# Seven products for eight in the gate's first 512 columns and in one more column group of the MLP's second product

## The chip, the core and the metric

The kernel runs on one core of one Trainium2 chip, as one launch. The metric is the device time in microseconds (us). Before the change three runs took 2023.22, 2023.70 and 2024.14 us, with a median of 2023.7 us.

## The reference

Two layers work on 256 tokens of width 2048, in float32 with weights in float32:

```python
for l in range(2):
    h = rms_norm(x, norm1_g[l])                    # 256 x 2048
    z = h @ w_in[l]                                # 2048 x 5120
    q, k, v, gu, gv = split(z, 5 parts of 1024)
    attn = dilated_attention(rotary(q), rotary(k), v)          # 8 heads of 128
    gm = gelu(gu) * spatial(layer_norm(gelu(gv)))              # 8 groups of 128
    x = x + concat(attn, gm) @ w_out[l]            # 2048 x 2048
    h2 = rms_norm(x, norm2_g[l])
    x = x + square(relu(h2 @ w_up[l])) @ w_down[l] # 2048 x 8192, 8192 x 2048
out = rms_norm(x, final_g)
```

`layer_norm` is over each group's 128 columns, and `spatial` a masked 128x128 mixing of tokens.

## The kernel before

**Weights and products.** Weights stream from HBM in pieces of 128x1024 (`Sub`, L150). ACT rounds a piece to fp32r (`hi`, L168) and DVE subtracts that from it (`lo`, L178); the moving side is split likewise, and each product is three matmuls: hi·hi, lo·hi, hi·lo. There are 7 buffers for raw pieces, 6 for `hi` and 6 for `lo`.

**Three kinds of step.** A `transposed` step takes one piece and issues 24 matmuls of 256 columns (L410). A `natural` step takes one piece and issues 12 matmuls of 512 columns (L470 to L472). A `fast` product (L414) covers 512 columns by 1024 rows with seven products of half size, as Strassen's scheme has it, in two block-steps of 42 matmuls of 256 columns each (L440). `transposed` steps need 96 matmuls of 256 columns for the same, `natural` ones 48 of 512. A block-step takes two pieces, `Top` and `Bottom`. ACT and DVE split their left halves (the `Top` one 512 wide, L186 and L191). DVE makes four sums of 512 from the raw pieces (L219, L220, L223, L224), called raw sums below, and these go through ACT and DVE as two further pieces, `Sums`: the "upper" one after the first two raw sums, the "lower" one after the other two. The moving side needs sums too: `sums` (L800) makes them with four DVE operations of 512, and `to_half` (L644) splits them with one ACT and one DVE operation of 512 for each pair of chunks. A block's products use the left half of `Top`, the left half of `Bottom`, the right half of `Bottom`, then the upper sums (twice), then the lower ones.

**Order.** The program is a list of steps. Each engine runs its instructions in the order in which they are emitted. Before a step come the `hi` of pieces up to four ahead and the `lo` of pieces up to four ahead, then its matmuls, then the work that its results start (`after`), and then what `later` has queued, within a budget. `soon` puts a call ahead of a later step, `hook` and `mark` behind a given one.

**The input product, in both layers.** First v (16 natural steps), then k and q of two heads at a time (columns of 256, four transposed steps each: k0, q0, k1, q1 and so on, 32 steps in all), then gv (16 natural steps) and gu (transposed). When a k or q is done, ACT swaps its halves (L577, L578) and DVE applies the rotary (L579 to L581). Two steps after a q, `scores` (L587) runs: PE L593 (called s1) and L596 (s0), DVE L602 and L604, ACT exp L606. `normalise` (DVE L611, ACT L614) and `turn` (PE L622, ACT L624) follow some steps later. gv goes through a gelu, then `stats` and `layer_norm` on POOL (L686, L690), then the mixing.

**The MLP.** In nine eighths e = 0 to 8, `w_up` of eighth e and `w_down` of eighth e-1 are emitted together. The table `ORDER` (and `USUAL` for the eighths that it doesn't name) says which 512-column groups of `w_down` go by seven products, a pair of numbers each, and at which of the eighth's steps the two blocks stand. e = 1 has two groups, most others three. `put` (L870) adds a group's products into a buffer in HBM by DMA.

Of the kernel before, what the change touches and what calls it, by code (L numbers as in the profile page):

```python
# [59 lines left out]

ORDER = {1: ((7, 10), (13, 14)), 6: ((12, 15), (2, 3), (7, 8)), 7: ((7, 10), (2, 3)), 8: ()}
FINAL = (7, 7, 6)
LAST = (4, 6, 8, 10, 0, 2, 12, 14)
USUAL = ((7, 9), (2, 3), (13, 14))
WARM = 11
HALVES = 5
BEHIND, BETWEEN = 2, 1
D_SCORES, D_NORM, D_TURN, D_VALUES = 2, 1, 3, 2  # L70


# [19 lines left out]
def trunk(ctx: ExitStack, tc: tile.TileContext, layout, xT, consts, gains, w, b_sp, w_sp, out):  # L92
# [9 lines left out]
    paux = ctx.enter_context(tc.tile_pool(name="paux", bufs=4, space=bass.MemoryType.PSUM))  # L102

    vec, act, pe = nc.vector, nc.scalar, nc.tensor

# [29 lines left out]
    def acc_bank(i=None, of=4):  # L135
# [2 lines left out]
            i = bank_at[0] = (bank_at[0] + 1) % of  # L138
        return pacc.tile([P, 512], F32, name=f"acc{i}", tag=f"acc{i}")

    def aux_bank():
        return paux.tile([P, 512], F32, name="aux", tag="aux")


    class Sub:
# [268 lines left out]
    def fast(name, l, row0, col0, tiles, slots, fresh, last, done):  # L414

        o = []  # L420
        for p in range(2):
            top, bottom = (cls(name, l, row0 + (4 * h + 2 * p) * P, col0, 2, 512) for h, cls in enumerate((Top, Bottom)))
            upper, lower = Sums(top, bottom, False), Sums(top, bottom, True)

            def mm(p=p, top=top, bottom=bottom, upper=upper, lower=lower):
                if p == 0:
                    o.extend(slots())
                half = tiles[0][0]
                sums_ready()
                extra = sum_parts[0]  # L430
# [44 lines left out]
    def mark(fn):  # L475

        steps.append((None, fn, None))

    def from_hs(k):
        return hs[:, k, :, :]  # L480
# [37 lines left out]
    def layer(l, n1, n2, n3, last):  # L518
# [26 lines left out]

        if l:
            mark(start)
        mix_a, mix_g = [None], [None]
        qk = {}
        turned = []  # L550
# [104 lines left out]


        def after_gv(c, ps):
            z, u = t32("gz", [2, 512], tag="tmpB"), t32("gu", [2, 512], tag="tmpA")
            for tt in range(2):
                act.activation(z[:, tt, :], ps[tt], AF.Copy, scale=n1.half[:, tt:tt + 1])  # L660

            def then(u, z):
# [5 lines left out]
                later(1, 1.5, lambda: stats(c // P))  # L668

            gelu(z, u, then)  # L670

        def stats(g0):
# [8 lines left out]
            later(0, 1.0, lambda: layer_norm(g0))  # L681

        def layer_norm(g0):
            y, mv = par["y"], par["mv"]
            r = t32("lr", [2, 4])
            rsqrt(nc.gpsimd, r, mv[:, :, g0:g0 + 4, 1], 1.0, LN_EPS, [2, 4])  # L686
            for g in range(4):
                for tt in range(2):
                    yg = y[:, tt, (g0 + g) * P:(g0 + g + 1) * P]
                    nc.gpsimd.tensor_scalar(yg, yg, mv[:, tt, g0 + g, 0:1], r[:, tt, g:g + 1],  # L690
                                            op0=OP.subtract, op1=OP.mult)
            par["normed"] += 4

        def spatial(g0):
# [44 lines left out]
        hook(base + d + 3, n1.factor)  # L739
        hook(base + d + 6, rope)  # L740
        hook(base + d + 8, shift)
        for j in range(4):
            transposed("w_in", l, 0, KC, AW + j * 256, 256, from_hs, lambda c, ps, j=j: after_qk("k", j, ps))
            transposed("w_in", l, 0, KC, j * 256, 256, from_hs, lambda c, ps, j=j: after_qk("q", j, ps))
        natural("w_in", l, 4 * AW, AW, after_gv)
# [35 lines left out]
        def after_up(e):  # L781
            def f(c, ps):
# [6 lines left out]
                    vec.scalar_tensor_tensor(z, pair(ps), 0.0, wide(n2.R), op0=OP.max, op1=OP.mult)  # L789
                act.activation(z, z, AF.Square)  # L790
                to_half(hid[e][0], c // P, z, True)
                if c == 768:
                    summed[0] = False
                    if e == 0:
                        new_shared(F32R)
                        sum_parts[0] = shared[0].rearrange("p (k h t) -> p k h t", k=NH, h=2)
                    later(1, 1.5, sums)
            return f

        def sums():  # L800

            a11, a12, a21, a22 = (inner[:, 4 * k:4 * k + 4, t * P:(t + 1) * P] for t in range(2) for k in range(2))
            vec.tensor_tensor(a22, a21, a22, op=OP.add)
            vec.tensor_tensor(a21, a11, a21, op=OP.subtract)
            vec.tensor_tensor(a11, a22, a11, op=OP.subtract)
            vec.tensor_tensor(a12, a12, a11, op=OP.subtract)

            def parts(k):
                to_half(sum_parts[0], k, inner[:, k:k + 2, :])
                summed[0] = k == 6  # L810

            for k in range(0, 8, 2):
                later(0, 0.6, lambda k=k: parts(k))

        def combine(place, c, banks, o=None):

# [32 lines left out]
        def halves(bank):  # L849
            return [bank[:, 0:256], bank[:, 256:512]]  # L850

        held = []

        def sevenths():
# [58 lines left out]
        for e in range(9):  # L913
# [1 line left out]
            if e == 8:  # L915
                mark(lambda: bank_at.__setitem__(0, 1))
            if e < 8:
                up = collect(transposed, "w_up", l, 0, KC, e * 1024, 1024, from_hs, after_up(e), of=2)
            if e:
                w = 512 * len(ORDER.get(e, USUAL))  # L920
                hidden = [hid[e - 1]]
                down = collect(transposed, "w_down", l, (e - 1) * 1024, 8, w, D - w, from_tiles(hidden, NH),
                               lambda c, ps, e=e, w=w: after_down(e, (c + w) // P, ps),
                               apart=last and e == 8, of=2 if e < 8 else 4,
                               cols=None if e < 8 else [c * P for c in LAST])
                for g, at in enumerate(ORDER.get(e, USUAL)):
                    banks = []
                    quick += zip(at, collect(fast, "w_down", l, (e - 1) * 1024, 512 * g, hidden,
                                             (lambda g=g, banks=banks: slots_other(g, banks)) if g else slots_first,
                                             (0, 2, 4, 6) if g or e == 1 else (6,), range(7) if g or e == 7 else (6,),  # L930
                                             other_done(e, g, banks) if g else first_done(e)))
# [144 lines left out]
```

## Time and profile before

| | before |
|---|---|
| median of 3 runs | 2023.7 us (2023.22 to 2024.14) |
| the profiled execution | 2023.7 us, of which its span is 2021.9 us |
| PE busy | 2009.5 us (99%) |
| DVE busy | 1579.8 us (78%) |
| ACT busy | 1221.2 us (60%) |
| POOL busy | 156.2 us (8%) |
| granted PE clock, mean | 0.997 |

The 1.8 us between the execution and its span lie around the span. A row of the timeline or the chain gives a start in us from the span's start, then a duration. A group's "mean ns of one" is longer than the pace of a run of such instructions, since the next one starts before the last has ended; so paces are taken from the starts of neighbouring rows, and PE's from the chain of waits, which counts the time to the next start.

### The profile page before, as it was taken

To read this page: it belongs to the slowest core of one execution; us is meant where nothing else is said; L and a number is where in the kernel's file an instruction comes from. 1 tells how busy PE (TensorE), PEld (TensorE's weight loads), DVE (VectorE), ACT (ScalarE), POOL (GpSimd) and SP (SyncE) were. 2 spreads that over 40 slices of the span, in tenths; PEclk is the share of its full clock that TensorE was granted. 3 is DMA by queue.
4 is the path that set the end of the run, shared out by engine and by line. 5 is a ranking of instruction groups with operands and counts; after the bars stand their busy time and mean duration, and the time that the engine had idled before them with its cause. 6 is when DMAs were issued, how large, how long until landed. Compare 5 with 4: busy or idle time off the path is not lost.

```text
span 2021.9 us, 40716 instructions
## 1 busy us (share of the span) xinstructions
PE 2009.5 (99%) x16810; PEld 1973.4 (98%) x16810; DVE 1579.8 (78%) x1954; ACT 1221.2 (60%) x1613; POOL 156.2 (8%) x200
## 2 busy tenths in 40 slices
PE   9999999999999999999999999999999999999997
PEld 8998999999999999999989989999999999999997
DVE  7566766688888898898856667667888898888985
ACT  7565455566566666665645654556666666667653
POOL 0002300000001000100000032000000000010000
PEclk9999999999999999999999999999999999999998
DMA  9555556566678776866664555565676776777662
GB/s 330 192 167 167 187 189 202 174 229 204 222 219 239 240 225 203 249 215 215 201 215 158 168 187 188 188 199 179 217 229 208 228 236 216 239 220 241 212 215 81
DMA packets 126442, 419.26 MB, mean 207 GB/s; under 512 B 14128, under 2 KB 22064, under 8 KB 126256
## 3 DMA queue, kind: packets, MB, share of 16 engines
q1 hardware_dynamic: 110800, 389.86, 57.2%
q0 software_dynamic: 14304, 23.86, 6.5%
q8 instruction: 131, 2.15, 0.4%
q10 hardware_dynamic: 1152, 2.94, 0.4%
q14 instruction: 55, 0.45, 0.1%
HBM read 394.58 MB, written 22.02 MB: 206 GB/s over the span
## 4 chain that ended last, share of the span: by engine, by line
PE 99%; DVE 0%; ACT 0%; issue 0%; DVEq 0%
PE acc L410 70%; PE acc L440 10%; PE aux L440 8%; PE acc L470 3%; PE acc L472 3%; PE acc L471 3%; PE aux L699 0%; PE aux L635 0%; PE aux L593 0%; PE aux L622 0%; PE aux L994 0%; DVE x L1038 0%; PE aux L596 0%; PE aux L637 0%; PE acc L846 0%; PE aux L539 0%
## 5 line engine op out<-in xcount | busy, mean ns | idle before, releaser
L168 ACT ACTIVATE hi<-raw 128x1024 fp32r<-128x1024 f32 (+1 forms) x817 | 836.9, 1050 | 487.5 <-DVE raw L220 216.2
L178 DVE TENSOR_TENSOR lo<-raw,hi 128x1024 fp32r<-128x1024 f32 (+1 forms) x817 | 965.3, 1214 | 143.4 <-ACT hi L168 140.4
L410 PE MATMUL acc<-hs,hi 128*128 128x256 f32 x5632 | 985.9, 277 | 0.0
L410 PEld LDWEIGHTS acc<-hs,hi 128*128 128x128 f32 x5632 | 857.9, 188 | 0.4 <-issue 0.2
L410 PE MATMUL acc<-hs,lo 128*128 128x256 f32 x2816 | 778.0, 276 | 0.0
L410 PEld LDWEIGHTS acc<-hs,lo 128*128 128x128 f32 x2816 | 528.7, 188 | 0.4 <-issue 0.2
L410 PE MATMUL acc<-half,hi 128*128 128x256 f32 x2688 | 462.2, 276 | 0.0
L410 PEld LDWEIGHTS acc<-half,hi 128*128 128x128 f32 x2688 | 406.7, 188 | 0.0
L410 PE MATMUL acc<-half,lo 128*128 128x256 f32 x1344 | 371.0, 276 | 0.0
L410 PEld LDWEIGHTS acc<-half,lo 128*128 128x128 f32 x1344 | 252.3, 188 | 0.0
L873 POOL DMA_DIRECT2D far<-ar x92 | 74.2, 816 | 1164.4 <-ACT ar L876 563.9
L440 PE MATMUL acc<-hi,shared 128*128 128x256 f32 x768 | 138.4, 276 | 0.0
L440 PEld LDWEIGHTS acc<-hi,shared 128*128 128x128 f32 x768 | 119.2, 188 | 0.0
L440 PE MATMUL aux<-hi,half 128*128 128x256 f32 x528 | 110.6, 276 | 0.0
L440 PE MATMUL acc<-lo,shared 128*128 128x256 f32 x384 | 106.0, 276 | 0.0
L649 DVE TENSOR_TENSOR half<-ar,half 128x512 fp32r<-128x512 f32 x72 | 49.8, 691 | 68.6 <-ACT half L646 68.6
L470 PE MATMUL acc<-hi,hs 128*128 128x512 f32 x256 | 101.8, 398 | 0.0
L472 PE MATMUL acc<-hi,hs 128*128 128x512 f32 x256 | 100.6, 393 | 0.0
L471 PE MATMUL acc<-lo,hs 128*128 128x512 f32 x256 | 100.3, 392 | 0.0
L440 PEld LDWEIGHTS aux<-hi,half 128*128 128x128 f32 x528 | 87.2, 188 | 0.0
L440 PE MATMUL aux<-hi,shared 128*128 128x256 f32 x448 | 80.7, 276 | 0.0
L510 DVE TENSOR_TENSOR x<-x,acc 128x512 f32<-128x512 f32 (+1 forms) x49 | 33.1, 675 | 59.1 <-PE acc L410 57.3
(150 smaller groups left out, 1955.3 us busy)
## 6 DMA issues: line engine op xcount, KB each, us to landing
raw<-in_w SPq DMA_DIRECT2D x731, 512.0 KB, 4.7
far<-ar POOLq DMA_DIRECT2D x60, 256.0 KB, 8.3
far<-ar POOLq DMA_DIRECT2D x32, 128.0 KB, 4.3
ar<-far POOLq DMA_DIRECT2D x12, 256.0 KB, 9.7
raw<-in_w SPq DMA_DIRECT2D x10, 256.0 KB, 5.1
x<-in_xT SPq DMA_DIRECT2D x7, 256.0 KB, 5.9
out<-x SPq DMA_DIRECT2D x7, 256.0 KB, 3.1
shared<-in_b_sp ACTq DMA_DIRECT2D x2, 512.0 KB, 7.7
```

What stands on the lines that cost most here:

```text
L168: act.activation(self.h[:, j * m:(j + 1) * m], self.raw[:, j * m:(j + 1) * m], AF.Copy)
L178: vec.tensor_tensor(lo[:, r], self.raw[:, r], self.h[:, r].bitcast(F32), op=OP.subtract)
L410: pe.matmul(o, lhsT=lhs, rhs=xs[:, rhs, :], start=(first and j == 0), stop=(last and j == 2), skip_group_check=True)
L440: calls.append(lambda k=k, j=j, lhs=lhs, rhs=rhs: pe.matmul(o[n], lhsT=lhs, rhs=rhs, start=(p == 0 and k == 0 and j == 0 and n in fresh), ...
L470: pe.matmul(ps, lhsT=xh, rhs=hi, start=(k0 + k == 0), stop=False)
L471: pe.matmul(ps, lhsT=xh, rhs=lo, start=False, stop=False)
L472: pe.matmul(ps, lhsT=xl, rhs=hi, start=False, stop=(k0 + k == KC - 1))
L510: vec.tensor_tensor(xj, xj, ps[j][:, 0:S] if alone else pair(ps)[:, j, :], op=OP.add)
L649: vec.tensor_tensor(t[:, c:c + 2, 1, :], src, t[:, c:c + 2, 0, :].bitcast(F32), op=OP.subtract)
L873: nc.gpsimd.dma_start(far[g][:, r], src, **({} if e == max(g, 1) else {"accum_op": OP.add}))
```

## The change

1. In the MLP, eighth e = 1 has three groups by seven products where it had two: `ORDER[1]` gets the pair (7, 8), and the first group's blocks stand at 2 and 5. The eighth e = 0 makes its hidden columns in the order 0, 512, 256, 768 and its sums in two halves, and `put` writes at e = 1 where it added.
2. In the input product of both layers the first 512 columns of gv go by seven products, in four block-steps of `fast`, two for each half of the rows. They stand among the 32 steps of k and q: ahead of the steps counted 3 and 6 (first rows) and 16 and 24 (second rows) from zero; they are called block 3, 6, 16 and 24 below. For the moving side, `seven_sums` makes scaled copies of x (8 on ACT, of 256) and four DVE sums of 512 (both called plain), once in v's steps and once behind step 3, ahead of step 4. `seven_parts` splits them, four times for each rows. The products are gathered after block 24 by `gather` and go through the gelu (`gate_half`) in the late natural steps, of which 8 are left. k and q use two PSUM banks, and s0 goes to the other of these.
3. The first four groups' `layer_norm` runs on DVE instead of POOL, and the last `turn` comes a step earlier.

Over the program there are 772 matmuls of 128x512 before and 580 after, and 15704 of 128x256 before and 16016 after. The core of the diff:

```diff
-ORDER = {1: ((7, 10), (13, 14)), 6: ((12, 15), (2, 3), (7, 8)), 7: ((7, 10), (2, 3)), 8: ()}
+ORDER = {1: ((2, 5), (7, 8), (13, 14)), 6: ((12, 15), (2, 3), (7, 8)), 7: ((7, 10), (2, 3)), 8: ()}
...
+SEVEN, AGAIN = ((3, 6), (16, 24)), 8
...
+    def strassen_sums(f, i, n):
+
+        a11, a12, a21, a22 = (f[:, 4 * k + i:4 * k + i + n, t * P:(t + 1) * P] for t in range(2) for k in range(2))
+        vec.tensor_tensor(a22, a21, a22, op=OP.add)
+        vec.tensor_tensor(a21, a11, a21, op=OP.subtract)
+        vec.tensor_tensor(a11, a22, a11, op=OP.subtract)
+        vec.tensor_tensor(a12, a12, a11, op=OP.subtract)
...
-            s1, s0 = aux_bank(), aux_bank()
+            s1, s0 = aux_bank(), acc_bank(1 - bank_at[0]) if aux_held else aux_bank()
...
-            later(D_TURN, 0.5, lambda: turn(j, p1, p0))
+            later(D_TURN - (j == 3), 0.5, lambda: turn(j, p1, p0))
...
+        def seven_sums(rows):
...
+            f = seven["plain"][rows]
+            for k in range(NH):
+                c = NH * rows + k
+                act.activation(f[:, k, :], x[:, c, :], AF.Copy, scale=g_all[:, n1.g, c:c + 1])
+            strassen_sums(f, 0, 4)
+
+        def seven_parts(rows, k):
+            to_half(seven["sums"], k, seven["plain"][rows][:, k:k + 2, :])
+
+        def seven_done(o):
+            soon(5, lambda: gather(o))
...
             r = t32("lr", [2, 4])
-            rsqrt(nc.gpsimd, r, mv[:, :, g0:g0 + 4, 1], 1.0, LN_EPS, [2, 4])
+            e = nc.gpsimd if g0 else vec
+            rsqrt(e, r, mv[:, :, g0:g0 + 4, 1], 1.0, LN_EPS, [2, 4])
...
+        hook(base + 13, lambda: seven_sums(0))
+        for k in range(0, NH, 2):
+            hook(base + 14 + k // 2, lambda k=k: seven_parts(0, k))
...
+        quick = {}
+        for rows in range(2):
+            quick.update(zip(SEVEN[rows], collect(fast, "w_in", l, 1024 * rows, 4 * AW, seven_forms(rows), seven_slots,
+                                                  () if rows else (0, 2, 4, 6), range(7) if rows else (),
+                                                  seven_done if rows else None)))
...
+        for i, one in enumerate(plain):
+            if quick.get(i):
+                steps.append(quick[i])
+            if i == 4:
+                mark(lambda: seven_sums(1))
+            if AGAIN < i <= AGAIN + 4:
+                mark(lambda k=2 * (i - AGAIN - 1): seven_parts(1, k))
+            steps.append(one)
+        late = collect(natural, "w_in", l, 4 * AW + 512, 512, lambda c, ps: soon(1, lambda: after_gv(512, ps)))
...
+                if e == 0 and c == 512:
...
+                    later(1, 1.0, lambda: sums([0]))
...
-            nc.gpsimd.dma_start(far[g][:, r], src, **({} if e == max(g, 1) else {"accum_op": OP.add}))
+            nc.gpsimd.dma_start(far[g][:, r], src, **({} if e == 1 else {"accum_op": OP.add}))
```

Below, rows of the two programs stand in the order in which the engine runs them; lines of after have the changed file's numbers (there `hi` is L173 and `lo` L183, the rotary L594 to L596, the plain sums L485 to L488, the raw sums L224 to L229, and `half<-plain` the splitting of sums, L661 and L664).

On DVE in layer 0, from the last raw pieces of v to the rotary of k0, before has:

```order
L178 TENSOR_TENSOR lo<-raw,hi 128x1024 x2
L543 SCALAR_TENSOR_TENSOR shared<-aux,cols,shared 128x128 x8
L178 TENSOR_TENSOR lo<-raw,hi 128x1024 x2
L579 TENSOR_TENSOR ar<-acc_565,cosR 128x512
L580 TENSOR_TENSOR ar<-ar,sinR 128x512
L581 TENSOR_TENSOR ar<-ar 128x512
L178 TENSOR_TENSOR lo<-raw,hi 128x1024 x4
```

and after has, from the raw sums of block 6 to the `lo` of its upper sums, the first of eight:

```order
L224 TENSOR_TENSOR raw<-raw 128x2x256
L225 TENSOR_TENSOR raw<-raw 128x2x256
L228 TENSOR_TENSOR raw<-raw 128x2x256
L229 TENSOR_TENSOR raw<-raw 128x2x256
L594 TENSOR_TENSOR ar<-acc_583,cosR 128x512
L595 TENSOR_TENSOR ar<-ar,sinR 128x512
L596 TENSOR_TENSOR ar<-ar 128x512
L485 TENSOR_TENSOR plain<-plain 128x4x128
L486 TENSOR_TENSOR plain<-plain 128x4x128
L487 TENSOR_TENSOR plain<-plain 128x4x128
L488 TENSOR_TENSOR plain<-plain 128x4x128
L183 TENSOR_TENSOR lo<-raw,hi 128x1024 x8
```

Block 6's raw sums now stand ahead of k0's rotary and the second rows' plain sums behind it, and the `lo` of block 6's upper sums behind both.

On ACT at the same place before has:

```order
L168 ACTIVATE hi<-raw 128x1024 x4
L577 ACTIVATE ar<-acc_565 64x512
L578 ACTIVATE ar<-acc_565 64x512
L168 ACTIVATE hi<-raw 128x1024 x4
L577 ACTIVATE ar<-acc_703 64x512
L578 ACTIVATE ar<-acc_703 64x512
```

and after has, from block 3's `Sums` on, with the eight scaled copies (L717) behind k0's two copies:

```order
L173 ACTIVATE hi<-raw 128x1024 x3
L191 ACTIVATE hi<-raw 128x512
L173 ACTIVATE hi<-raw 128x1024 x2
L592 ACTIVATE ar<-acc_583 64x512
L593 ACTIVATE ar<-acc_583 64x512
L717 ACTIVATE plain<-x,cols 128x256 x8
L173 ACTIVATE hi<-raw 128x1024 x8
L592 ACTIVATE ar<-acc_807 64x512
L593 ACTIVATE ar<-acc_807 64x512
```

What moved: k0's copies stand behind the `hi` of block 6's upper sums, and that waits for DVE's raw sums.

On DVE behind the first scores of layer 0, before has:

```order
L178 TENSOR_TENSOR lo<-raw,hi 128x1024
L611 RECIPROCAL den<-den 128x4
L178 TENSOR_TENSOR lo<-raw,hi 128x1024
L579 TENSOR_TENSOR ar<-acc_829,cosR 128x512
L580 TENSOR_TENSOR ar<-ar,sinR 128x512
L581 TENSOR_TENSOR ar<-ar 128x512
L178 TENSOR_TENSOR lo<-raw,hi 128x1024 x4
```

and after has, from k1's rotary to q1's, with block 16's pieces in between:

```order
L183 TENSOR_TENSOR lo<-raw,hi 128x1024
L594 TENSOR_TENSOR ar<-acc_999,cosR 128x512
L595 TENSOR_TENSOR ar<-ar,sinR 128x512
L596 TENSOR_TENSOR ar<-ar 128x512
L664 TENSOR_TENSOR half<-plain,half 128x2x256
L196 TENSOR_TENSOR lo<-raw,hi 128x512
L183 TENSOR_TENSOR lo<-raw,hi 128x1024
L224 TENSOR_TENSOR raw<-raw 128x2x256
L225 TENSOR_TENSOR raw<-raw 128x2x256
L228 TENSOR_TENSOR raw<-raw 128x2x256
L229 TENSOR_TENSOR raw<-raw 128x2x256
L183 TENSOR_TENSOR lo<-raw,hi 128x1024 x2
```

Block 16's raw sums and the `lo` of both its `Sums` stand between the two rotaries, and what block 16's next step waits for stands behind the second.

## Rows read from the trace of the kernel before

**Rows 1.** Page, part 1 and the start of part 4: busy time; chain that ended last.

```profile
PE 2009.5 (99%) x16810; PEld 1973.4 (98%) x16810; DVE 1579.8 (78%) x1954; ACT 1221.2 (60%) x1613; POOL 156.2 (8%) x200
...
PE 99%; DVE 0%; ACT 0%; issue 0%; DVEq 0%
```

**Rows 2.** Windows: stretch, length, busy us (instructions) of each engine, clock, DMA.

```profile
50.00:250.00 200.00, 200.00 (x1522) 190.01 (x1521) 131.56 (x191) 110.17 (x164) 30.87 (x42) 1.00 0.55 178
390.00:560.00 170.00, 170.00 (x1501) 170.00 (x1500) 145.91 (x165) 108.84 (x135) 9.56 (x15) 1.00 0.65 213
```

**Rows 3.** Chain, layer 0: start us, us, what.

```profile
57.07 1.72 PE aux L539 x4
...
81.88 11.31 PE acc L410 x96
93.19 0.65 PE aux L622 x6
93.84 10.90 PE acc L410 x96
```

**Rows 4.** Chain in the MLP: a seven-product block.

```profile
466.61 4.08 PE acc L440 x36
```

**Rows 5.** Timeline of PE, first natural steps: start us, us, instruction.

```profile
7.87 0.39 PE L470 MATMUL acc<-hi,hs 128*128 128x512 f32 x1
...
11.99 0.39 PE L470 MATMUL acc<-hi,hs 128*128 128x512 f32 x1
```

**Rows 6.** Timeline of DVE in the MLP: the four raw sums and what follows.

```profile
469.61 0.69 DVE L219 TENSOR_TENSOR raw<-raw 128x512 f32<-128x512 f32 x1
...
472.39 2.52 DVE L178 TENSOR_TENSOR lo<-raw,hi 128x1024 fp32r<-128x1024 f32 x2
```

**Rows 7.** Lines by form, POOL: busy us, mean ns of one.

```profile
L690 POOL TENSOR_SCALAR shared<-shared,mv,lr 128x128 f32<-128x128 f32 x32 | 39.6, 1248 | 0.4
```

**Rows 8.** Timeline of DVE, layer 0, before and after the first steps on k.

```profile
45.08 4.63 DVE L178 TENSOR_TENSOR lo<-raw,hi 128x1024 fp32r<-128x1024 f32 x4
...
52.20 0.42 DVE L567 TENSOR_TENSOR cosR<-con,aux 128x256 f32<-128x256 f32 x1 [2.49 <-ACT nR L333]
...
52.94 2.36 DVE L178 TENSOR_TENSOR lo<-raw,hi 128x1024 fp32r<-128x1024 f32 x2
...
57.97 2.16 DVE L543 SCALAR_TENSOR_TENSOR shared<-aux,cols,shared 128x128 f32<-128x128 f32 x8 [2.67 <-PE aux L539]
```

**Rows 9.** Timeline of ACT: one pair of scaled copies of x.

```profile
300.35 0.91 ACT L287 ACTIVATE hs<-x,cols 128x256 fp32r<-128x256 f32 x2 [2.33 <-DVE x L510]
301.17 0.62 ACT L300 ACTIVATE nsq<-x 128x512 f32<-128x512 f32 x1
```

**Rows 10.** Timeline of ACT, layer 1: copies of q, then probabilities.

```profile
1064.77 0.60 ACT L577 ACTIVATE ar<-acc 64x512 f32<-64x512 f32 x1 [1.66 <-PE acc L410]
...
1083.41 0.51 ACT L606 ACTIVATE ar<-ar,mx 128x256 f32<-128x256 f32 x1 [3.97 <-DVE mx L604]
...
1085.18 1.04 ACT L168 ACTIVATE hi<-raw 128x1024 fp32r<-128x1024 f32 x1
1086.13 1.48 ACT L614 ACTIVATE ar<-ar,den 128x256 f32<-128x256 f32 x4
1087.52 1.04 ACT L168 ACTIVATE hi<-raw 128x1024 fp32r<-128x1024 f32 x1
```

**Rows 11.** Timeline of DVE, layer 1: rotary of q, then scores.

```profile
1066.02 0.69 DVE L579 TENSOR_TENSOR ar<-acc,cosR 128x512 f32<-128x512 f32 x1 [4.37 <-ACT ar L578]
...
1067.95 4.62 DVE L178 TENSOR_TENSOR lo<-raw,hi 128x1024 fp32r<-128x1024 f32 x4
...
1081.96 0.69 DVE L602 SCALAR_TENSOR_TENSOR ar<-aux,con 128x512 f32<-128x512 f32 x1 [0.72 <-PE aux L593]
...
1084.08 1.21 DVE L178 TENSOR_TENSOR lo<-raw,hi 128x1024 fp32r<-128x1024 f32 x1
```

**Rows 12.** Windows: near the end of the program.

```profile
2010.00:2015.00 5.00, 1.17 (x4) 0.88 (x4) 3.66 (x10) 0.00 (x0) 0.00 (x0) 0.57 0.26 86
```

More of the change, by code (lines that the diff above doesn't have):

```diff
@@ L101, in trunk @@
     pacc = ctx.enter_context(tc.tile_pool(name="pacc", bufs=1, space=bass.MemoryType.PSUM))
-    paux = ctx.enter_context(tc.tile_pool(name="paux", bufs=4, space=bass.MemoryType.PSUM))
+    paux = ctx.enter_context(tc.tile_pool(name="paux", bufs=1, space=bass.MemoryType.PSUM))
     vec, act, pe = nc.vector, nc.scalar, nc.tensor
@@ L139, in acc_bank @@
         return pacc.tile([P, 512], F32, name=f"acc{i}", tag=f"acc{i}")
+    aux_at, aux_held = [3], set()
     def aux_bank():
-        return paux.tile([P, 512], F32, name="aux", tag="aux")
+        i = next(j % 4 for j in range(aux_at[0] + 1, aux_at[0] + 5) if j % 4 not in aux_held)
+        aux_at[0] = i
+        return paux.tile([P, 512], F32, name=f"aux{i}", tag=f"aux{i}")
     class Sub:
@@ L412, in transposed, with fast @@
             steps.append((wt, mm, (lambda c=c: after(c, accs[c])) if k0 + 4 == nk else None))
-    def fast(name, l, row0, col0, tiles, slots, fresh, last, done):
+    def fast(name, l, row0, col0, forms, slots, fresh, last, done):
         o = []
@@ L427, in mm @@
                     o.extend(slots())
-                half = tiles[0][0]
-                sums_ready()
-                extra = sum_parts[0]
+                half, extra = forms()
                 left, right = slice(0, 256), slice(256, 512)
@@ L477, in mark, with halves @@
         steps.append((None, fn, None))
+    def strassen_sums(f, i, n):
[4 more added lines that the diff above has]
+        vec.tensor_tensor(a12, a12, a11, op=OP.subtract)
+    def halves(bank):
+        return [bank[:, 0:256], bank[:, 256:512]]
     def from_hs(k):
@@ L667, in then, with seven_slots @@
                 vec.scalar_tensor_tensor(par["y"][:, :, c:c + 512], u, 1.0, z, op0=OP.add, op1=OP.mult)
-                later(1, 1.5, lambda: stats(c // P))
+                if c:
+                    later(1, 1.5, lambda: stats(c // P))
+                else:
+                    stats(0)
             gelu(z, u, then)
+        seven = {}
+        def seven_slots():
+            if "o" not in seven:
+                banks = [acc_bank(2), acc_bank(3)]
+                for _ in range(2):
+                    banks.append(aux_bank())
+                    seven.setdefault("aux", []).append(aux_at[0])
+                aux_held.update(seven["aux"])
+                seven["o"] = [h for b in banks for h in halves(b)][0:7]
+            return seven["o"]
@@ new lines, in seven_forms @@
+        def seven_forms(rows):
+            return lambda: (hs[:, NH * rows:NH * (rows + 1)], seven["sums"])
+        def seven_sums(rows):
+            if "sums" not in seven:
+                f = tp.tile([P, 2, NH, S], F32, name="plain", tag="half", bufs=2)
+                seven["plain"] = [f[:, i, :, :] for i in range(2)]
+                seven["sums"] = tp.tile([P, NH, 2, S], F32R, name="half", tag="half", bufs=2)
+            f = seven["plain"][rows]
[3 more added lines that the diff above has]
+            strassen_sums(f, 0, 4)
@@ new lines, in seven_parts, with gather @@
+        def seven_parts(rows, k):
+            to_half(seven["sums"], k, seven["plain"][rows][:, k:k + 2, :])
+        def seven_done(o):
+            soon(5, lambda: gather(o))
+        def gather(o):
+            z = t32("gz", [2, 512], tag="tmpB")
+            p1, p2, p3, p5, p7, p6, p4 = o
+            c11, c12, c21, c22 = (z[:, tt, h * S:(h + 1) * S] for tt in range(2) for h in range(2))
+            act.activation(c12, p1, AF.Copy)
+            vec.tensor_tensor(c11, c12, p2, op=OP.add)
+            vec.tensor_tensor(c12, c12, p6, op=OP.add)
+            vec.tensor_tensor(c22, c12, p7, op=OP.add)
+            vec.tensor_tensor(c12, c12, p5, op=OP.add)
+            vec.tensor_tensor(c21, c22, p4, op=OP.subtract)
+            vec.tensor_tensor(c12, c12, p3, op=OP.add)
+            vec.tensor_tensor(c22, c22, p5, op=OP.add)
+            for tt in range(2):
+                act.activation(z[:, tt, :], z[:, tt, :], AF.Copy, scale=n1.half[:, tt:tt + 1])
+            aux_held.clear()
+            seven["z"] = z
@@ L680, in stats @@
                     vec.bn_aggr(mv[:, tt, g0 + g, :], st[:, tt, g, :])
-            later(0, 1.0, lambda: layer_norm(g0))
+            if g0:
+                later(0, 1.0, lambda: layer_norm(g0))
+            else:
+                soon(1, lambda: layer_norm(0))
         def layer_norm(g0):
@@ L741, in layer @@
         hook(base + d + 8, shift)
+        hook(base + 13, lambda: seven_sums(0))
+        for k in range(0, NH, 2):
+            hook(base + 14 + k // 2, lambda k=k: seven_parts(0, k))
+        plain = []
         for j in range(4):
-            transposed("w_in", l, 0, KC, AW + j * 256, 256, from_hs, lambda c, ps, j=j: after_qk("k", j, ps))
-            transposed("w_in", l, 0, KC, j * 256, 256, from_hs, lambda c, ps, j=j: after_qk("q", j, ps))
-        natural("w_in", l, 4 * AW, AW, after_gv)
+            for name, col in (("k", AW), ("q", 0)):
+                plain += collect(transposed, "w_in", l, 0, KC, col + j * 256, 256, from_hs,
+                                 lambda c, ps, j=j, name=name: after_qk(name, j, ps), of=2)
+        quick = {}
[3 more added lines that the diff above has]
+                                                  seven_done if rows else None)))
+        if l:
+            mark(lambda: bank_at.__setitem__(0, 1))
+        for i, one in enumerate(plain):
[7 more added lines that the diff above has]
+        late = collect(natural, "w_in", l, 4 * AW + 512, 512, lambda c, ps: soon(1, lambda: after_gv(512, ps)))
+        for i, one in enumerate(late):
+            if i == 5:
+                mark(lambda: gate_half(0, seven["z"]))
+            steps.append(one)
         transposed("w_in", l, 0, KC, 3 * AW, AW, from_hs, after_gu)
@@ L791, in f, with sums @@
                 to_half(hid[e][0], c // P, z, True)
+                if e == 0 and c == 512:
+                    new_shared(F32R)
+                    sum_parts[0] = shared[0].rearrange("p (k h t) -> p k h t", k=NH, h=2)
+                    later(1, 1.0, lambda: sums([0]))
                 if c == 768:
                     summed[0] = False
[L794 to L797, printed above, removed]
-            return f
[L800 to L806, printed above, removed]
+                    later(1, 1.5, lambda: sums([0, 1] if e else [1]))
+            return f
+        def sums(ps):
+            strassen_sums(inner, 2 * ps[0], 2 * len(ps))
             def parts(k):
@@ L812, in sums @@
             for k in range(0, 8, 2):
-                later(0, 0.6, lambda k=k: parts(k))
+                if k % 4 // 2 in ps:
+                    later(0, 0.6, lambda k=k: parts(k))
         def combine(place, c, banks, o=None):
@@ L917, in layer @@
             if e < 8:
-                up = collect(transposed, "w_up", l, 0, KC, e * 1024, 1024, from_hs, after_up(e), of=2)
+                up = collect(transposed, "w_up", l, 0, KC, e * 1024, 1024, from_hs, after_up(e), of=2,
+                             cols=None if e else (0, 512, 256, 768))
             if e:
```

17 lines of the change are left out of this document (11 added, 6 removed).

## The prediction

> **What bounds the kernel now.** I read the page first. PE is busy for 2009.5 of 2021.9 us, DVE for 78% and ACT for 60%, and the chain of work that ended last is PE for 99% [rows 1]. So a matmul that is saved is worth its pace, as long as nothing else becomes late. Next the windows. In the stretch of layer 0 that holds k, q and gv, PE is busy for 200.00 of 200.00 us, DVE for 131.56 (66%) and ACT for 110.17 (55%). In a stretch of the MLP in which most column groups go by seven products already, PE is busy for all of 170.00 us beside a DVE at 145.91 (86%) [rows 2]. The reader is to see that a fuller DVE doesn't by itself stop PE. It stops PE where a chain of DVE and ACT work ends later than PE comes to it, which is why the rest goes by places.
>
> **The matmuls.** The chain gives the pace of 256-column matmuls: 96 in 10.90 us, 0.1135 us each [rows 3]. In a seven-product block 36 take 4.08 us, the same 0.113 [rows 4], so a block of 42 takes 4.77 and a transposed step of 24 takes 2.725. The natural steps' 512-column matmuls start 18 apart between 7.87 and 11.99 us, 0.2289 each [rows 5]. The gate loses 96 of these per layer, 21.97 us, and gets 168 of 256 columns, 19.07 us: 2.90 us saved, 5.8 in two layers. The new group in the MLP has 84 matmuls for 96 per layer: 12 x 0.1135, in two layers 2.7. In sum 192 x 0.2289 - 312 x 0.1135 = 43.95 - 35.41 = **8.5 us saved**. Against the profiled execution's own 2023.7 us (a span of 2021.9 and 1.8 around it; the median of the runs is 2023.7 too) that gives 2015.2.
>
> **What DVE gets.** Per layer the k, q and gv stretch gets, on DVE, 16 raw sums, 8 plain sums and 8 splittings of 512 (0.695 each, four raw sums taking 2.78 us [rows 6]: 22.2 us), 4 `lo` of 1024 net (1.16 each, four in 4.63 [rows 8]: 4.6) and 4 of 512 (at 0.69, 2.8), and about 7.5 us of gathering and layer norm: 37 us. In 200 us that lifts DVE from 66% to 84%. The layer norm of four groups leaves POOL, where one operation takes 1.25 us [rows 7]. On DVE no row has it; L543, also of 128x128, took 2.16 / 8 = 0.27 us each [rows 8], and I take that. At POOL's price the 8 would take 10 us, at worst 7.8 us more of DVE, far from any matmul. The weights loaded are the same bytes. The raw pieces are held longer, but PE waits nowhere for a load in these windows, and I cost this at nothing.
>
> **Place 1: block 6 in layer 0.** From 45.08 us [rows 8], when DVE has ended the first norm, the new order has 10 `lo` of 1024 (11.6 us), 2 of 512 (1.4), 16 operations of 512 (11.1), cos and sin (0.74, from 52.20 to 52.94) and L543's eight (2.16) until block 6's raw sums are done: 27.0 us, so 72.1, if it never waits. Its upper two are done at 70.7. ACT then makes their `hi` (0.95 to 1.04 [rows 10], 71.7), k0's two copies (1064.77 to 1066.02 for q in layer 1, 1.25 [rows 10, 11], to 72.9) and the eight scaled copies. A pair of these moves the next start by 0.82 us [rows 9], so eight take 3.3: 76.2. Only then can DVE make the plain sums (2.78, to 79.0) and the `lo` of the upper sums (1.16, to 80.1). PE's own time: step 2 starts at 58.79 (57.07 and 1.72 more [rows 3]), step 2, block 3 and steps 3 to 5 bring it to 58.79 + 4 x 2.725 + 4.77 = 74.45, and after 19 matmuls of block 6 (2.16) it wants that `lo` at 76.6. It waits **3.5 us**. A DVE without the backlog would leave place 2's 0.9; if DVE also waits for ACT on the way, 4.5.
>
> **Place 2: block 6 in layer 1.** Here the first norm is done early and DVE has no backlog. Let step 3 end at e. k0's copies end at e + 1.25, with the `hi` of block 6 partly in front at e + 1.8. Eight copies: e + 5.1; plain sums: e + 7.9; `lo`: e + 9.0. PE wants it after steps 4 and 5 and 19 matmuls, at e + 7.6. It waits **1.4 us**; 0.9 if the `hi` isn't in front, 2.0 if all of it is.
>
> **Place 3: the step behind block 16, both layers.** The clock starts when s1 is done (1081.96 in layer 1 [rows 11]). PE then has s0 (0.44), six steps (16.35, of which four run 0.41 slower in before: 11.31 for 10.90), a turn (0.66 [rows 3]), block 16 (4.77), and two left-over matmuls and one of its own ahead of the first that needs the step's `lo`: 22.9. On DVE: the scores end at 2.1 [rows 11], a `lo` at 3.3. The splitting of sums waits for ACT, whose exps end at 3.2 (1085.18 less 1081.96 [rows 10]) and which makes a `hi` before its own part: 4.8, so DVE is at 5.6 with the reciprocal. A `lo` to 6.8. The next splitting waits for L614's four (1.39 to the next start [rows 10]), a `hi` and its ACT part: 8.6, done 9.3. A `lo`, k1's rotary (1066.02 to 1067.95, 1.93 [rows 11]), the last splitting, a `lo` of 512 and one of 1024: 14.9. Raw sums: 17.7, the upper `lo` 18.8. The lower `hi` on ACT stands behind the turn's copies and ends at 19.1, its `lo` at 20.3. On ACT one more `hi` and q1's two copies follow: 21.3. Then q1's rotary on DVE, 23.2, and the `lo` that PE wants, **24.4: 1.5 us late**, in each layer. If q1's copies could follow PE's last matmul (17.9) at once, they would end at 19.1 and nothing would be late; with the prices of single instructions for those of runs, it is up to 2.5.
>
> **The other places.** Behind each of these waits of PE stand only PE's own later matmuls; DVE and ACT don't wait for them in the next 5 us and catch up meanwhile, so the waits add up and don't spread. Block 3 is met with about 1 us to spare in layer 0, block 24 and the step behind it with 0.5, by the same count (the halves' splitting is over by then, which relieves DVE of 0.7 us in each of four steps, and ACT of as much). Behind block 24 the gather's 1 copy, 7 additions and 2 scalings stand off PE's path, with 2 us to spare at the next natural steps. In the MLP the pairs (2, 5), (7, 8) and (13, 14) put 9 us more on DVE in one eighth (8 raw sums, 2 `lo` of each width), a load which rows 2 show elsewhere with PE busy throughout: I cost them at 0, at most 1.5 us per layer. POOL issues 8 more DMAs for the third group, on a queue that is busy for 8% of the span [rows 1]; 0. `put` without adding, s0's other bank and the hidden columns' new order change no count on PE; 0.
>
> **The sum.** 2023.7 - 8.5 + 3.5 + 1.4 + 2 x 1.5 = **2023.1 us**. Bounds: 2015.2 + 0.9 + 0.9 = 2017.0 with only the smallest waits, 2015.2 + 4.5 + 2.0 + 5.0 + 3.0 = 2029.7 with the largest.
>
> **Rivals.** A, the waits are mostly hidden, with 0.9 left at places 1 and 2 and none at place 3: 2015.2 + 1.8 = **2017.0**. For it: DVE at 86% in the MLP beside a PE that never waits [rows 2], and queued work that runs ahead of what my counts allow; against it, places 1 and 2 hold a chain of k0's copies, eight copies and four sums in which only the 1.3 us of the `hi` and the backlog can shrink.
>
> B, slower: DVE's backlog isn't worked off between the blocks. Each of the waits on ACT in place 3 pushes the raw sums, they push the next `hi`, and the next block starts late too. Then place 1 costs 4.5, block 3 of layer 0 another 1.0, place 2 costs 2.0, and blocks 16 and 24 cost 2.0 each in both layers, 8.0: 2015.2 + 15.5 = **2030.7**. It decides from the point where the `lo` behind block 24 is over 0.5 us later than counted. For it: DVE's 84% with three engines taking turns; against it, the queues have 4.8 us of a block's matmuls to catch up in, and in the MLP they do.
>
> C, the clock falls in place 1. Before holds PE at a granted clock of 1.00 in both windows, where it never idles [rows 2]; between 2010 and 2015 us, where it works for 1.17 of 5.00, the mean is 0.57, a stretch at the lower level (1.2 of 2.4 GHz) for the most part [rows 12]. No row has a wait of 3.5 us in the midst of work. If the 23 matmuls left in block 6 ran at half pace, that is 2.6 us more: **2025.7**; half pace through the next step would add 2.7. The Trainium skill ("TensorE: Matmul & The Clock Gate", section on oscillation in real kernels) says that a wait of the matmul engine that is long enough halves its clock, and that what follows starts slow each time. By it, C's 2025.7 would hold if the wait is long enough; the trace agrees as far as its end goes.
>
> **How the numbers follow.** A difference of 0.2%, 4 us, is about what a measurement tells from no change, so faster is under 2019.7 and slower over 2027.7. My forecast with its neighbours, 2019.7 to 2025.5: 0.37. C: 0.06, also within. A and what lies between it and the forecast's lower side: 0.34. B with the upper bounds: 0.23. So faster 0.34, same 0.43, slower 0.23. The range goes from 2015.2, nothing late, to 2029.5; 0.05 lies below, 0.12 above. The forecast's own range is 2019.5 to 2026.
>
> **What would show it.** The waits of PE would name DVE's `lo` as releaser, with some 3.5 us once in layer 0 near 77 us and about 1.5 us at three more places; the chain would pass over the scaled copies and plain sums at block 6. PE's busy time should fall by 8.5 us, that of DVE rise by some 80. The forecast is wrong if PE has no wait over 1 us (A), or if waits of over 1 us stand at block 24 or behind (B), or if the granted clock falls below 1.00 near 80 us (C).

## The result, and the profile after

The change made the kernel slower: 2028.94 us median (2026.49 to 2030.13, 11 runs) against 2023.47 us of before; the ratio is 1.0026, with a 95% interval of 1.0018 to 1.0033. The forecast was 2023.1. Before's median is over 11 runs too, one of which took 5273.57 us, while the other ten lie between 2023.16 and 2024.14. The profiled execution has a span of 2028.4 us, 6.5 more than before's. At 2030.13 us it is the slowest of after's 11 runs, 1.2 us over their median, so what is read from it below adds up to that run and not to the median.

The page's first part, with busy time, share and instructions of each engine, answers to [rows 1]:

```profile
PE 2008.5 (99%) x16930; PEld 1979.2 (98%) x16930; DVE 1659.2 (82%) x2108; ACT 1258.8 (62%) x1695; POOL 136.8 (7%) x166
```

DVE is at 82% where it was at 78%: 79 us more, as forecast. PE's busy time has fallen by 1.0 us only, not 8.5, so its matmuls take longer too. The waits of PE, by what released it (us in total, times, longest):

```profile
PE acc L443 <- DVE lo L183: 6.3, 2, 3.3
PE aux L608 <- DVE ar L596: 1.2, 2, 0.6
```

Both lines are new. The first is block 6, once in each layer; the second is the first scores, once in each layer.

Where the 6.5 us come from can be read from one landmark, the first matmul of `w_out`. It starts at 244.12 us in before and at 249.03 in after: layer 0's input product is 4.9 us longer where 2.9 were to be saved, so 7.8 us are lost there. In layer 1 it starts 8.1 us late, after 3.6 at that layer's first norm (1018.07 and 1021.66): 4.5 longer, 7.4 lost. In between, the MLP gives back 1.3 us, and from layer 1's landmark to the end of the span 1.6: its 12 matmuls (1.36 us), in full.

**Block 6, 5.0 us in layer 0.** The chain of after there (start us, us, what):

```profile
74.58 1.39 PE acc L443 x13
...
75.99 0.70 DVE plain L485
...
78.17 0.04 DVE plain L488
...
78.78 1.23 DVE lo L183
...
80.05 0.84 PE acc L443 x5
80.89 2.94 PE aux L443 x16
83.83 0.21 PE acc L415
84.05 0.43 PE aux L443 x2
84.47 5.52 PE acc L415 x47
```

PE runs dry, and the chain goes over DVE's plain sums and the upper `lo`, which ends at 80.0. The prediction had 80.1. From 74.58 to 84.47 are 43 matmuls, counting six that ran beside the plain sums, 4.88 us at 0.1135; they took 9.89. Of the 5.0 us, 3.3 are the wait. The other 1.7 lie behind it: the last 24 matmuls took 80.05 to 84.47, 4.42 us for 2.72, at up to 0.21 us each, and then the pace is 0.1135 again. The window there (length, busy us of PE, PEld, DVE, ACT and POOL, clock):

```profile
80.00:84.40 4.40, 4.35 (x25) 4.35 (x26) 4.40 (x4) 1.75 (x2) 0.00 (x0) 0.65 0.65 196
```

The granted clock is 0.65 in this stretch, part of it at the lower level of 1.2 GHz, after 3.3 us in which PE did nothing. It doesn't fall with the restart: the matmuls up to 81.18 still start 0.11 to 0.12 us apart (the first two 0.22), those from 81.29 on 0.21. In layer 1 the same block took 4.9 us too long, 3.0 by the wait and 1.9 behind it.

**The first scores, 1.0 us.** The chain of layer 0 behind block 6:

```profile
93.32 1.13 PE aux L608 x4
94.45 0.45 PE acc L611 x4
94.89 13.62 PE acc L415 x120
108.52 0.66 PE aux L637 x6
109.17 5.46 PE acc L415 x48
114.63 2.72 PE acc L443 x24
```

s1 starts at 93.32; 71 matmuls after 84.47 would have brought it to 92.5, and its four take 1.13 us where they take 0.87 in the other scores. Then come 120 matmuls, a turn and 48 more before block 16 at 114.63: seven steps, not six.

**The pace, 1.4 us.** One place of before has 96 matmuls in 11.31 us [rows 3]. The chain of after, later in layer 0:

```profile
124.91 11.31 PE acc L415 x96
136.22 0.65 PE aux L637 x6
136.88 8.48 PE acc L415 x72
```

That is 0.1178 each, at a granted clock of 1.00. In before it holds for 96 matmuls of each layer, in after for some 420, from block 16's end to the last scores: 420 x 0.0043 = 1.8 us for 0.4. The three together are 7.4 of the 7.8 us.

### The profile page after: what moved, and what is told of

Its sections match the earlier page's. It is cut to its first block, busy times and chain, and to the rows that moved or that the text cites. A ratio compares the mean times of both kernels' runs of the same rounds, so it can differ in the third digit from the quotient of the medians.

```text
span 2028.4 us, 41171 instructions
## 1 busy us (share of the span) xinstructions
PE 2008.5 (99%) x16930; PEld 1979.2 (98%) x16930; DVE 1659.2 (82%) x2108; ACT 1258.8 (62%) x1695; POOL 136.8 (7%) x166
## 4 chain that ended last, share of the span: by engine, by line
PE 98%; DVE 1%; DMA 1%; ACT 0%; issue 0%; ACTq 0%; DVEq 0%; SPq 0%
PE acc L415 69%; PE acc L443 11%; PE aux L443 9%; PE acc L475 2%; PE acc L473 2%; PE acc L474 2%; PE aux L608 0%; PE aux L774 0%; PE aux L650 0%; DMA raw<-in_w 0%; PE aux L637 0%; DMA x<-in_xT 0%; DVE x L1138 0%; PE aux L652 0%; PE acc L943 0%
## 5 line engine op out<-in xcount | busy, mean ns | idle before, releaser
L173 ACT ACTIVATE hi<-raw 128x1024 fp32r<-128x1024 f32 (+1 forms) x829 | 844.9, 1049 | 450.4 <-DVE raw L225 263.0
L183 DVE TENSOR_TENSOR lo<-raw,hi 128x1024 fp32r<-128x1024 f32 (+1 forms) x829 | 980.6, 1215 | 109.1 <-ACT hi L173 105.1
L415 PE MATMUL acc<-half,hi 128*128 128x256 f32 x2560 | 440.5, 276 | 0.0
L415 PEld LDWEIGHTS acc<-half,hi 128*128 128x128 f32 x2560 | 387.4, 188 | 0.0
L415 PE MATMUL acc<-half,lo 128*128 128x256 f32 x1280 | 353.3, 276 | 0.0
L415 PEld LDWEIGHTS acc<-half,lo 128*128 128x128 f32 x1280 | 240.3, 188 | 0.0
L443 PE MATMUL aux<-hi,half 128*128 128x256 f32 x608 | 128.0, 279 | 0.0
L664 DVE TENSOR_TENSOR half<-ar,half 128x512 fp32r<-128x512 f32 x72 | 49.7, 691 | 63.7 <-ACT half L661 63.7
L443 PEld LDWEIGHTS aux<-hi,half 128*128 128x128 f32 x608 | 101.3, 190 | 0.0
L443 PE MATMUL acc<-hi,half 128*128 128x256 f32 x480 | 91.7, 276 | 0.0
L443 PE MATMUL aux<-lo,half 128*128 128x256 f32 x304 | 84.8, 279 | 0.0
L443 PEld LDWEIGHTS acc<-lo,shared 128*128 128x128 f32 x416 | 78.1, 188 | 0.0
```

The lines of the kernel that those rows point to most:

```text
L173: act.activation(self.h[:, j * m:(j + 1) * m], self.raw[:, j * m:(j + 1) * m], AF.Copy)
L183: vec.tensor_tensor(lo[:, r], self.raw[:, r], self.h[:, r].bitcast(F32), op=OP.subtract)
L415: pe.matmul(o, lhsT=lhs, rhs=xs[:, rhs, :], start=(first and j == 0), stop=(last and j == 2), skip_group_check=True)
L443: calls.append(lambda k=k, j=j, lhs=lhs, rhs=rhs: pe.matmul(o[n], lhsT=lhs, rhs=rhs, start=(p == 0 and k == 0 and j == 0 and n in fresh), ...
L664: vec.tensor_tensor(t[:, c:c + 2, 1, :], src, t[:, c:c + 2, 0, :].bitcast(F32), op=OP.subtract)
```

## The experiments

All kernels are compared with runs of before on the same chip.

**Only the MLP's part**, with the gate as before. Of the edit this is the table's line, cut short; the columns' order, the split sums and `put` go with it:

```diff
-ORDER = {1: ((7, 10), (13, 14)),
+ORDER = {1: ((2, 5), (7, 8), (13, 14)),
```

> Only the first part of the change: the third group at e = 1 with its places, the hidden columns' order, the split sums and put. The gate is as before. It saves 24 matmuls of 0.1135 us: 2.7 us faster than before, 2020.8, if nothing in that eighth is late, as the prediction had it. If the fuller eighth makes PE wait, it is between 2021 and 2024.

Measured: 2020.64 us (2020.00 to 2021.07), ratio 0.9985 (0.9977 to 0.9994). Its profile has no wait of PE that before lacks. 2.9 us saved for 2.7 forecast: this part is what it seems.

**Only the gate's part:**

> Only the gate's seven products: ORDER and put are as before, the rest as after. If the third group at e = 1 gives its 12 matmuls per layer in full (2.7 us), this is slower than after by 2.7 us, 2031.6. If it waits somewhere for what it saves, this equals after, 2029.

Measured: 2030.51 us (2028.34 to 2034.00, 5 runs), ratio 1.0036 (1.0023 to 1.0049). 1.6 us over after, within the spread of both, so this one doesn't tell 2.7 from 0; the one before does. But its profile, which is of the fastest of the five runs, shows a second thing. The same place in layer 0, chain and window:

```profile
78.88 1.23 DVE lo L183
...
80.16 0.86 PE acc L443 x5
81.01 1.88 PE aux L443 x16
82.90 0.12 PE acc L415
83.01 0.24 PE aux L443 x2
```

```profile
80.00:84.40 4.40, 4.24 (x36) 4.25 (x37) 4.40 (x5) 2.66 (x3) 0.00 (x0) 1.00 0.69 210
```

The wait is the same 3.3 us, the clock is 1.00, and the 24 matmuls behind it take 3.10 us where after's took 4.42. In layer 1 they take 3.09 where after's took 4.61, at a clock of 1.00 again. So of the 1.7 and 1.9 us behind after's waits, some 0.4 each come with a restart at full clock, and 1.3 and 1.5 with the fall of the clock. The same wait is followed by a slow stretch in one execution and not in another. Both can happen within one execution: s0_in_aux below has block 6's waits of 3.3 and 3.0 us too, and these are the windows behind them, in layer 0 and in layer 1:

```profile
80.00:84.40 4.40, 4.32 (x36) 4.32 (x37) 4.40 (x5) 2.62 (x3) 0.00 (x0) 1.00 0.66 194
1083.70:1088.30 4.60, 4.23 (x24) 4.23 (x25) 4.60 (x5) 2.07 (x3) 0.00 (x0) 0.68 0.64 192
```

Seven profiles of this case have a wait of 2.0 to 3.3 us in each layer. Of these 14 waits, seven are followed by a granted clock below 1.00: both in after and sums_at_7, one in s0_in_aux, scores_late and sums_7_scores_late, none in gate_only and sums_at_3. The times go with the clock: gate_only's run of 2028.34 us has a mean clock of 0.998, its run of 2034.00 one of 0.995. The kernels here in which PE waits for 2.0 to 3.3 us at a time have runs that spread over 3.6 to 6.0 us (one of them, s0_in_aux below, over 0.7); those with shorter waits or none over 1.0 to 2.4.

**The second rows' sums behind block 6:**

```diff
-            if i == 4:
+            if i == 7:
                 mark(lambda: seven_sums(1))
```

> The second rows' scaled copies and plain sums are made behind block 6 (at step 7) instead of ahead of step 4; the rest is as after. Theory 1 (block 6's upper lo waits because these eight copies and four sums stand ahead of it, and PE then runs at half clock for the rest of the block): PE's waits of 3.3 and 3.0 us at block 6 go, the granted clock stays 1.00 there, and the time falls by the 4.9 + 4.8 us that block 6 costs in after, to about 2019. Theory 2 (DVE has too much to do in this stretch, wherever the sums stand): the wait moves to q0's rotary and the scores, 3 us or more in each layer, and the time stays between 2024 and 2029.

Measured: 2022.21 us (2020.51 to 2026.54), ratio 0.9994 (0.9985 to 1.0003). Block 6's wait is gone, 6.7 us with it. What is left of PE's waits in this stretch:

```profile
PE aux L608 <- DVE ar L596: 4.5, 2, 2.3
```

The wait has moved to the first scores and grown from 0.6 to 2.3 us each, and the clock falls behind both. The time lies between the two forecasts. So far this speaks for both theories: the sums' place costs the time at block 6, and the work is late elsewhere.

**The sums ahead of step 3** (`if i == 3`):

> The same copies and sums are made ahead of step 3, so ahead of k0's copies and of block 6's raw sums. Theory 1 in its narrow form (they hurt only because they stand behind k0's copies, which wait for PE): block 6's wait falls below 1 us in both layers, no half clock, about 2019 to 2021. Theory 2 (DVE's backlog): the raw sums of block 6 come 2.8 us later and PE still waits 2 to 4 us in layer 0, less in layer 1 where there is no backlog: 2022 to 2026.

Measured: 2025.82 us (2025.15 to 2031.14), ratio 1.0014 (1.0006 to 1.0023). PE waits 2.0 us at block 6 in each layer and up to 1.4 at the step behind block 3. This is theory 2's forecast, but for the layers: they are alike, so DVE is behind in layer 1 too.

**The splittings one step later**, alone and with the sums at 7:

```diff
-SEVEN, AGAIN = ((3, 6), (16, 24)), 8
+SEVEN, AGAIN = ((3, 6), (16, 24)), 9
```

> Only the four splittings one step later (AGAIN 9); the sums stay ahead of step 4, as in after. Block 6 keeps its waits of 3.3 and 3.0 us; the waits at the first scores (0.6 us in each layer, with some 0.3 of slower matmuls) go: some 1.8 us off 2028.9, about 2027. If the scores' place were no matter, 2029.

> The sums behind block 6 as in sums_at_7, and the four splittings of the second rows one step later (AGAIN 9). Each splitting in after is a step of its own without a weight, and queued work runs behind it too, so the splitting ahead of step 9 lets the first scores run one step (2.7 us) early. Theory 1 (the order costs the time, not the amount of DVE work): the scores come 2.7 us later, the waits of 2.3 us on q0's rotary go, no clock falls, and the time is 2015 to 2018. Theory 2 (DVE has too much to do here): the wait turns up again at block 16 or behind it, and the time stays at 2020 to 2024.

Alone: 2027.76 us (2026.35 to 2031.37), ratio 1.0022 (1.0013 to 1.0031). The scores' waits are gone, and 1.2 and 1.5 us of wait have come up at the step behind block 16, in layers 0 and 1. The time alone doesn't tell this kernel from after, the intervals overlap; the profile does. With the sums at 7: 2022.54 us (2020.48 to 2024.88), ratio 0.9993 (0.9984 to 1.0002). Its chain in layer 0, from the first scores on:

```profile
91.30 0.86 PE aux L608 x4
92.17 0.44 PE acc L611 x4
92.61 8.48 PE acc L415 x72
101.09 0.65 PE aux L637 x6
101.75 8.18 PE acc L415 x72
109.92 2.05 PE acc L443 x18
...
112.36 0.60 ACT ar L592
...
112.97 0.60 ACT ar L593
...
113.60 0.69 DVE ar L594
114.29 0.61 DVE ar L595
...
115.53 1.23 DVE lo L183
...
116.81 4.13 PE acc L415 x23
```

Now six steps lie between the scores and block 16, and PE waits 2.0 us for the `lo` behind q1's rotary, by way of q1's copies (112.36), the rotary (113.60) and that `lo` (115.53): place 3 of the prediction, step by step. The time lies in theory 2's range, and at this point theory 2 looks better.

**The sums ahead of step 11:**

> The copies and sums ahead of step 11, behind the first scores, and the splittings ahead of steps 12 to 15, close to block 16. Theory 1: nothing late at block 6 or at the first scores, but the work now stands just ahead of block 16's raw sums; by my count for place 3 (1.5 us late with the sums done early) that makes block 16 or its next step 2 us late or more in each layer: 2019 to 2022. If DVE has more room there than I counted, 2015 to 2017.

Measured: 2025.34 us (2024.97 to 2027.32), ratio 1.0012 (1.0003 to 1.0021). PE waits for the last splittings at block 16, 1.7 us in each layer, and up to 1.6 behind it. Worse than forecast by 3 us.

**The second rows' blocks later**, with the sums at 7 and AGAIN 9:

```diff
-SEVEN, AGAIN = ((3, 6), (16, 24)), 9
+SEVEN, AGAIN = ((3, 6), (18, 26)), 9
```

> As sums_7_scores_late, with the second rows' blocks ahead of steps 18 and 26 instead of 16 and 24. In sums_7_scores_late PE waits 2.0 us in each layer in the step behind block 16, for a lo that stands behind q1's rotary on DVE, which stands behind the block's raw sums and both Sums' lo: place 3 of the prediction. Ahead of step 18, q1's copies end 5 us before the block. Theory 1 (order): the 4.0 us and the slower matmuls behind them go, and nothing else gets late: 2016 to 2018.5, faster than both kernels. Theory 2 (amount): the scores of the next heads, which then come right at the block, are late or hold the block up: 2020 to 2024.

> The same with the blocks ahead of steps 17 and 25. q1's copies end 2.3 us before the block. Theory 1: the chain of place 3 has 2.7 us more room for its 2.0 us of lateness, so the wait goes or stays below 0.5 us: 2016 to 2019. Theory 2: 2020 to 2024.

Blocks at 17 and 25: 2021.18 us (2020.41 to 2021.83), ratio 0.9988 (0.9980 to 0.9997), with 1.3 and 0.7 us of wait in the blocks themselves and four of up to 0.3 behind them. That is in theory 2's range, and theory 1's 0.5 is missed: one step isn't enough room. Blocks at 18 and 26: **2018.21 us** (2017.96 to 2018.95), ratio 0.9975 (0.9965 to 0.9985), faster than both kernels. All waits of PE in its profile are the two at the program's ends, which before has too:

```profile
PE aux L333 <- DVE nr L359: 1.2, 1, 1.2
PE aux L1094 <- DVE warm L1090: 1.1, 1, 1.1
```

And the window that answers to [rows 2], first in this kernel, then in after:

```profile
50.00:250.00 200.00, 200.00 (x1604) 193.91 (x1603) 165.24 (x256) 122.74 (x189) 17.55 (x21) 1.00 0.54 180
50.00:250.00 200.00, 196.07 (x1551) 189.54 (x1550) 160.25 (x249) 119.30 (x185) 17.58 (x21) 0.99 0.52 172
```

DVE is busy for 165 of 200 us, more than in after (160), and PE for all of them. Over the program both kernels have the same 2108 DVE instructions, busy for 1659 us. That decides against theory 2: the amount fits, and PE waited for where it stood, on DVE and ACT and against PE's own blocks. The third part of the change, the layer norm on DVE and the earlier turn, was not run alone, but this kernel has it too. The runs lie within 1 us. What is left over 2015.2 is, by the count, the pace: the chain has some 490 matmuls (58 us; 54 in the expectation of s0_first below) per layer at 0.1178, 2.2 us more than at 0.1134, less before's 0.4. In two layers that is 3.5 us, and 2015.2 + 3.5 = 2018.7, 0.5 over the measured time.

**What sets the pace.** In this kernel it sets in behind the first scores:

```profile
90.91 0.44 PE acc L611 x4
91.36 8.48 PE acc L415 x72
```

Two kernels were to tell by what. The first puts s0 into another bank (`aux_bank()`, as before), the second emits s0's matmuls ahead of s1's in the kernel just shown.

> s0 goes to one of the two free aux banks again instead of the other of k's and q's banks. In after the 256-column matmuls run at 0.1178 us instead of 0.1134 from block 16's end to the last scores, about 1.0 us per layer more than before. If that is tied to the bank that s0 uses, the pace is 0.1134 in that stretch and the time falls by some 2 us to 2027; if it isn't, nothing changes (2029), or it is slower where turn and scores then wait for a free bank.

> As blocks_18_26, with PE making s0 (four matmuls of 128 columns) ahead of s1 (of 256) in each scores. In blocks_18_26 PE waits nowhere, and what is left over 2015.2 is a pace of 0.1178 us instead of 0.1134 in about 54 us per layer (2.0 us each, of which before has 0.4); it sets in right behind s0's matmuls at the first scores. If the narrow matmuls just ahead of the weights' matmuls bring it about, it doesn't set in here and the time is 2015 to 2016. If not, it stays at 2018.2, perhaps 0.4 us more where DVE gets s1 later.

s0 in the other bank: 2030.01 us (2029.53 to 2030.25), ratio 1.0032 (1.0019 to 1.0044), with the same 96 matmuls in 11.31 us and 2.2 us of new waits for a free bank. s0 first: 2018.33 us (2017.77 to 2018.73), ratio 0.9974 (0.9964 to 0.9984), with 72 matmuls in 8.48 us behind the first scores as well. Neither of the two causes is it. The slow pace can also end: in sums_at_7's profile, where PE waited just ahead of the first scores, it is missing from there on, and scores_late has it behind the first scores but no longer behind its wait at block 16:

```profile
97.59 8.48 PE acc L415 x72
...
126.53 10.90 PE acc L415 x96
```

What brings it about stays open.

## Why the prediction was wrong

- **The savings** were right: 2.7 us in the MLP (2.9 measured), and the gate's 5.8 as far as the kernel that waits nowhere shows it, in which the slow pace takes some 3 us back.
- **Place 1** was right in mechanism and size: 3.5 us forecast, 3.3 measured, by the same chain.
- **Place 2** was mis-sized: 1.4 us forecast, 3.0 measured. The step that failed is "Here the first norm is done early and DVE has no backlog". DVE in layer 1 (start us, us):

```profile
1053.51 0.69 DVE L485 TENSOR_TENSOR plain<-plain 128x512 f32<-128x512 f32 x1 [4.67 <-ACT plain L717]
...
1065.05 5.76 DVE L183 TENSOR_TENSOR lo<-raw,hi 128x1024 fp32r<-128x1024 f32 x5
...
1072.46 0.68 DVE L224 TENSOR_TENSOR raw<-raw 128x512 f32<-128x512 f32 x1
1073.18 0.69 DVE L225 TENSOR_TENSOR raw<-raw 128x512 f32<-128x512 f32 x1
```

There was indeed no backlog from the norm: DVE stood idle for 4.67 us before 1053.51, waiting for the first rows' scaled copies. But from their plain sums on it has no pause over 0.31 us until block 6's raw sums, which it reaches at 1072.46, behind seven `lo` in a row. Step 3 ended at 1073.1 (1078.55 less two steps), and ACT:

```profile
1073.98 1.07 ACT L173 ACTIVATE hi<-raw 128x1024 fp32r<-128x1024 f32 x1 [3.83 <-DVE raw L225]
1075.08 0.59 ACT L592 ACTIVATE ar<-acc 64x512 f32<-64x512 f32 x1
1075.68 0.59 ACT L593 ACTIVATE ar<-acc 64x512 f32<-64x512 f32 x1
1076.30 3.31 ACT L717 ACTIVATE plain<-x,cols 128x256 f32<-128x256 f32 x8
```

The `hi` waits for the second raw sum, and k0's copies start 2.0 us after the step's end, not at once or after half a `hi`. The whole `hi` in front was the upper bound I gave, a wait of 2.0 us; with raw sums that late it is more.

- **Place 3** was no cost in after: 3.0 us forecast, 0 measured. The step that failed is "six steps": the scores come one step earlier in after, because a splitting is a step of its own, behind which the queue is served. With six steps the wait is there: 1.2 and 1.5 us with the sums at 4 and 2.0 with the sums at 7, for 1.5 forecast. The early scores cost 1.0 us per layer instead, a term the prediction doesn't have.
- **The clock**, rival C, was put at nothing in the sum, with a chance of 0.06 and for layer 0 alone. In this execution it fell in both layers. Behind the waits stand 1.7 and 1.9 us, of which the clock is 1.3 and 1.5 by the comparison with gate_only; C's 2.6 took half pace for all 23 matmuls, and the first ten still ran at the full one. The restart at full clock, some 0.4 us each time, is in no term.
- **The pace** of 0.1178, 1.4 us per layer more than in before, was in the rows, as 11.31 us for 96 matmuls, and I took it as staying where it was, without a reason.

In sum, 3.3 + 3.0 + 0 us of waits at the three places, 3.6 behind these waits by the clock and the restart, 2.0 at the scores and 2.8 of pace make 14.7, where the prediction had 7.9; the landmarks give 15.2. The largest misses are thus two terms at nothing, the clock and the pace. The time lies in the range, near its top, but no change was forecast and the kernel is slower by 0.26%. That it lies in the range at all is partly luck: the 3.0 us counted at place 3, which after doesn't have, stand in for others that weren't counted. B, the rival on that side, isn't what happened: blocks 16 and 24 were not late. C's mechanism is, with place 2, the scores and the pace beside it; its time, 2025.7, isn't.

## What to carry to other kernels

When work is put into the queues of engines that another waits for, count where it stands, not only how much it is: here the same instructions cost 10.7 us more or less by their places (2028.94 and 2018.21 us), with the faster kernel's DVE the fuller one. Count the steps between two events in the order that was built, since a step without work of its own can let queued work run early. And price a wait of the matmul engine of 2 us or more above its length, and expect that price to vary from run to run: half of such waits here were followed by a lower clock.

## What the runs showed of the hardware

A wait of 3.3 us was followed by about 4.4 us at a mean clock of 0.65 in one execution, and by a clock of 1.00 in another kernel's execution with the same wait at the same place (4.42 and 3.10 us for the same 24 matmuls). Waits of 2.0 us (sums_7_scores_late, layer 0) and 2.3 us (sums_at_7, both layers) were followed by a lower clock too, so the length of the wait alone doesn't decide. The Trainium skill ("TensorE: Matmul & The Clock Gate", part 1) says that the window by which the clock is judged runs freely, and that the point at which the clock rises varies because it depends on where in the window a kernel's first matmul lands. If a pause is taken the same way, which is my inference, the same wait can end either way; the 14 waits agree with that, but no profile here shows the window.

With the granted clock at 1.00, 256-column matmuls run at 0.1134 or at 0.1178 us for tens of microseconds on end, and natural ones at 0.2289 or 0.2333 (24 from 176.22 to 181.82 in after): 0.0044 us more per matmul, whatever its width. In the profiles here the pace changes only where other matmuls (scores, a turn), a block's end or a wait stand in between, and it can change either way. Neither s0's bank nor the order of s0 and s1 decides it.
